# Priority for the copies of a four-chunk recurrence, and two pinned VectorE steps, in a hybrid decoder layer

## The chip, the cores and the metric

One core of one Trainium2 chip runs one layer of a decoder for a prompt of 256 tokens and 8 single-token samples together (264 columns). The metric is the device time of the kernel in microseconds (us). The engines of the core run side by side, each through its own queue in a fixed order: TensorE (PE in the profile), VectorE (DVE), ScalarE (ACT), GpSimd (POOL), and SyncE (SP), which here only issues transfers.

## What is computed

The layer is a half-step SwiGLU network, a mixing stage, and a second half-step network. The mixing stage has windowed attention for half of the width and an RWKV-7 recurrence for the other half. The change touches the recurrence alone:

```python
def step(S, inp):
    r_t, lw_t, k_t, v_t, kk_t, a_t = inp
    sa = jnp.einsum('bhij,bhj->bhi', S, -kk_t)
    S = (S * jnp.exp(lw_t)[:, :, None, :] + sa[..., None] * (kk_t * a_t)[:, :, None, :]
         + v_t[..., None] * k_t[:, :, None, :])
    return S, jnp.einsum('bhij,bhj->bhi', S, r_t)
```

16 heads of width 64 run through it. The rest of the layer is matrix products in float32 accuracy: `x + 0.5 * swiglu(norm(x))`, then `x + mixed @ w_out`, then the second network.

## The kernel before

Every weight product is made of *chunks* of 128 x 512 weights (`chunk` and `gemm`). SyncE loads a chunk into `raw` (6 buffers); ScalarE casts it to `hi`; VectorE subtracts it to get `lo` (4 buffers each; in a part of the mixing stage GpSimd makes every second `lo`). TensorE then makes 12 products of 128 x 264 per chunk into an accumulator `acc`, three for each of the chunk's four tiles: `hi` by the high part of the activations, `hi` by the low part, `lo` by the high part. So a `lo` that comes late stops TensorE, and because VectorE works in order, so does whatever stands ahead of that `lo` in VectorE's queue.

The recurrence is done in four chunks of 64 tokens, for two pairs of heads at a time: four *batches*, each a generator (`chain`). The generators advance by one `yield` with each weight chunk of the mixing stage (`tick`), so that their small instructions are traced between the chunks. For each batch:

1. Once `prep` has written the masked products `gm` to a DRAM scratch (`sa`), `chain` loads them back as `X` and `Xt` (`Y` in the code), waits 8 steps, and inverts 32 x 32 triangles on VectorE: for s = 1 to 30 a product `st` and an addition into `Xt`, each addition waiting for its product and each product for the addition before it. These 60 instructions are called the *inverse* below.
2. `Xt` goes to DRAM (`sb`) and comes back as `TT`; after 8 more steps two VectorE transpositions make `TN` from it.
3. TensorE multiplies with `TN`, ScalarE copies the result (`zs`), TensorE multiplies again, ScalarE copies into `TT`.
4. TensorE makes `pW` and `pU`. ScalarE copies `pW` to `W`; VectorE copies one half of `pU` to `uv`, ScalarE the other half. TensorE makes `pP`, `pG` from `W` and `pN`, `pY` from `uv`. ScalarE copies `pP` to `PT`; VectorE adds `pG` into `KR` (`kr`) and scales `pN` into `N`.
5. Three steps over the chunks, c = 1, 2, 3: TensorE multiplies the state `S` (at first a part of `N`) by `PT`; VectorE makes `Z`, then the next `S`.

The order in which instructions stand on each engine is not the traced one: a scheduler with its own timeline model orders them, by priority and by when it takes them to be ready. `tc.high_priority()` raises the instructions in its block; the loads, casts and `lo` of the weight chunks have it already. `tc.keep_in_program_order(i)` forbids that `i` stands ahead of the instruction that was traced before it on its engine. The inverse of one batch runs on VectorE at about the time at which the steps 3 to 5 of the batch before it run on the other engines.

Of the kernel before, what the change touches and what calls it, by code (L numbers as in the profile page):

```python
# [10 lines left out]
ALU = mybir.AluOpType  # L11
AX = mybir.AxisListType

P = 128
# [10 lines left out]
HALF = (slice(0, 64), slice(64, 128))  # L25
# [8 lines left out]
DWAIT = (8, 8, 8, 8)  # L34
# [13 lines left out]
def body(tc, I, O):  # L48
    nc = tc.nc
    V, A, G, TE, SP = nc.vector, nc.scalar, nc.gpsimd, nc.tensor, nc.sync  # L50
# [6 lines left out]
    def tt(e, out, a, b, op):  # L57
        return e.tensor_tensor(out=out, in0=a, in1=b, op=op)  # L58

    def stt(out, a, s, b, op0, op1):  # L60
        return V.scalar_tensor_tensor(out=out, in0=a, scalar=s, in1=b, op0=op0, op1=op1)  # L61
# [8 lines left out]
    def bc(ap, shape):  # L70
        return ap.broadcast_to(list(shape))

    def mm(out, lhsT, rhs, start=True, stop=True, **k):
        TE.matmul(out, lhsT, rhs, start=start, stop=stop, **k)  # L74
# [16 lines left out]
    def pause(n):  # L91
        for _ in range(n):
            yield

    with ExitStack() as ctx:
# [14 lines left out]
        def acc():  # L110
            return pp.tile([P, 512], F32, tag="acc", bufs=NACC, name=uid("acc"))

        def mp():
            return pp.tile([P, 512], F32, tag="m", bufs=NM, name=uid("m"))
# [243 lines left out]
        def mixing_body(mx, n2, n3, XD):  # L358
            def fix(shape, name):
                return mx.tile(list(shape), F32, name=name)  # L360

            def ring(shape, tag, bufs):
                return mx.tile(list(shape), F32, tag=tag, bufs=bufs, name=uid(tag))
# [9 lines left out]
            wc = fix((P, NPAIR, 4), "wc")  # L373
# [18 lines left out]
            def win(t):  # L392
                ps = acc()
                gemm(ps, I["win"][t], n2.xs, tick, share=t >= LKV + 4)
                if not have[0]:
                    n2.rstd(rs)
                    have[0] = True
                return ps
# [141 lines left out]
            def newbatch(i):  # L540
                bt = Batch()
                n = BATCH[i]
                bt.i, bt.n, bt.left, bt.p0 = i, n, n, sum(BATCH[:i])
                bt.KR, bt.bv = [None] * n, [None] * n
                bt.Gm = [[None, None] for _ in range(n)]
                bt.BT = [None] * n
                bt.UV = ring((P, 4, n, P), "uv", NUV)
                return bt

            def chain(bt):  # L550
                n = bt.n
# [7 lines left out]
                X = ring((ng * nr, 32, 32), "X", 1)  # L559
                Y = ring((ng * nr, nj, 32), "Xt", 1)  # L560
# [4 lines left out]
                TT = ring((P, n * 4, 64), "TT", NTT)  # L565
# [3 lines left out]
                for s in range(1, 31):  # L569
                    m, w = -(-s // ng), 31 - s  # L570
                    t = ring((ng * nr, m, w), "st", 2)
                    shp = (ng * nr, m, w)
                    tt(V, t, bc(X[:, s:s + 1, s + 1:], shp), bc(Y[:, :m, s:s + 1], shp), ALU.mult)
                    tt(V, Y[:, :m, s + 1:], Y[:, :m, s + 1:], t, ALU.add)
                    if s % NSTEP == 0:
                        yield
# [6 lines left out]
                for h in range(2):  # L583
                    for blk in range(2):
                        x = h * 64 + blk * 32
                        SP.dma_start(TT[x:x + 32, :, blk * 32:blk * 32 + 32],
                                     scr2[bt.i].rearrange("(h b m) (s t) -> h b s m t", h=2, b=2, s=32)[h, blk])
                yield from pause(DWAIT[bt.i])
                TN = ring((P, n * 4, 32), "TN", 1)
                for h in range(2):  # L590
                    V.transpose(TN[h * 64:h * 64 + 32], TT[h * 64:h * 64 + 32, :, 0:32])
                yield
                def sub(h, x):
                    return slice(h * 64 + x * 32, h * 64 + x * 32 + 32)
# [1 line left out]
                def quads(k):  # L596
                    return slice(k * 4, k * 4 + 4), slice(k * P, k * P + P)

                ps = mp()
# [7 lines left out]
                for k in range(n):  # L607
                    c, x = quads(k)
# [3 lines left out]
                ps = mp()  # L612
# [5 lines left out]
                for k in range(n):  # L618
                    c, x = quads(k)
# [4 lines left out]
                uv = bt.UV  # L624
                W, PT = ring((P, n, 3, 64), "W", 1), ring((P, n, 3, 64), "PT", 1)
                N = ring((P, n, 4, 64), "N", 1)
                pW, pU = mp(), mp()
# [6 lines left out]
                                    mm(ps[HALF[h ^ m], j * 64:j * 64 + 64], TT[HALF[h], j, :],  # L634
                                       bt.KR[k][HALF[h], a, c, :])
                pW, pU = (ps.rearrange("p (k c t) -> p k c t", k=n, c=4) for ps in (pW, pU))
                A.copy(W, pW[:, :, 1:4, :])
                V.tensor_copy(uv[HALF[0], :, :, HALF[0]].rearrange("p c k t -> p k c t"), pU[HALF[1]])
                A.copy(uv[HALF[1], :, :, HALF[1]].rearrange("p c k t -> p k c t"), pU[HALF[0]])
                yield  # L640
                pP, pG = mp(), mp()
                for k in range(n):
# [6 lines left out]
                            r = HALF[h]  # L649
                            mm(pG[r, x:x + 64], W[r, k, c - 1, :], bt.Gm[k][h][r, c, 64:128])  # L650
                pP, pG = (ps[:, :n * 192].rearrange("p (k c t) -> p k c t", k=n, c=3) for ps in (pP, pG))
                for h in range(2):
                    A.copy(PT[HALF[h]], pP[HALF[1 - h]])
                for k in range(n):
                    tt(V, bt.KR[k][:, 1, 1:4, :], pG[:, k], bt.KR[k][:, 1, 1:4, :], ALU.add)
                pN, pY = mp(), mp()
                for k in range(n):
                    for c in range(4):
# [4 lines left out]
                for k in range(n):  # L663
                    for c in range(4):
                        x = (k * 4 + c) * 64
                        for h in range(2):
                            r = HALF[h]
                            mm(pY[HALF[1 - h], x:x + 64], uv[:, c, k, r], bt.Gm[k][h][:, c, 64:128],
                               k + c == 0, c == 0, skip_group_check=True)
                tt(V, N, pN[:, :n * 256].rearrange("p (k c t) -> p k c t", k=n, c=4),  # L670
                   bc(wc[:, bt.p0:bt.p0 + n, :].unsqueeze(3), (P, n, 4, 64)), ALU.mult)
                yield
                S = N[:, :, 0, :]
                for c in range(1, 4):
                    ps = mp()
                    for k in range(n):
                        for h in range(2):
                            r = HALF[h]
                            mm(ps[r, k * 64:k * 64 + 64], PT[r, k, c - 1, :], S[r, k])
                        for h in range(2):  # L680
                            r = HALF[h]
                            x = (k * 4 + c) * 64
                            mm(pY[HALF[1 - h], x:x + 64], S[r, k], bt.KR[k][r, 1, c, :], False, True,
                               skip_group_check=True)
                    Z, Sn = ring((P, n, 64), "Z", 2), ring((P, n, 64), "S", 3)
                    for k in range(n):
                        stt(Z[:, k], S[:, k], wc[:, bt.p0 + k, c:c + 1], N[:, k, c, :], ALU.mult, ALU.add)
                    for k in range(n):
                        stt(Sn[:, k], ps[:, k * 64:k * 64 + 64], wc[:, bt.p0 + k, c:c + 1], Z[:, k], ALU.mult, ALU.add)
                    S = Sn  # L690
                    yield
                for k in range(n):
# [12 lines left out]
                for k in range(n):  # L705
                    p, o = bt.p0 + k, Ys[k]
# [169 lines left out]
            for kind, i in SEQ:  # L876
                if kind == "b":
                    bt = newbatch(i)
                    for k in range(BATCH[i]):
                        p = bt.p0 + k  # L880
                        x = [shifted(2 + 3 * p + j, tmp()) for j in range(3)]
                        spawn(prep(p, bt, k, *x))
                    bat.append(spawn(chain(bt)))
                    bts.append(bt)
                    if len(bat) == len(BATCH):
                        A.dma_start(O["sh"], shc)
                elif kind == "kv":
                    w, p = i // 2, i % 2
                    ps = win(LKV + i)
# [5 lines left out]
                else:  # L895
                    ps = win(LKV + 4 + i)
# [5 lines left out]
                    if i % 4 == 3:  # L902
                        p = i // 4
# [20 lines left out]
            for pi, ks in enumerate(PASS):  # L924
# [5 lines left out]
                for o in range(KD):  # L930
                    ps = acc()
# [160 lines left out]
```

## Time and profile before

| | us |
|---|---|
| three runs | 2001.56, 2002.91, 2004.8 |
| profiled execution, its own time | 2001.57 |
| its span, first to last instruction | 1999.8 |
| TensorE busy in the span | 1969.5 |
| VectorE busy | 1301.4 |
| ScalarE busy | 1065.4 |

The profiled execution is the fastest of the runs; what lies around its span is 1.8 us. The first network ends at about 769 us, and the mixing stage ends at about 1235 us. The views that follow are parts of the profile's page, the waits, sums over windows of time, and timelines of one engine. A timeline's row has the start in us, the duration in us, engine, line, operation, what is written and what is read, the shape, and how many equal instructions the row holds; in brackets stands the idle time of the engine before it and what ended that. TensorE's rows overlap, since its products are pipelined: how long a group holds the engine is read from its start to the next group's start. A program matmul of float32 operands shows as two rows' worth of instructions in the profile (x2), one of the `acc` products as one.

### The profile page before, as it was taken

Reading aid. Unit: us, or ns where it says so; the run is one execution under the profiler, and the core shown is the slowest. Engines: PE = TensorE matmul, PEld = TensorE weight load, DVE = VectorE, ACT = ScalarE, POOL = GpSimd, SP = SyncE. Lnnn points to the kernel's source line nnn. Section 1 sums busy time; section 2 is a strip of 40 time slices with the busy share of each in tenths; the row PEclk is TensorE's granted clock in tenths of the full one; section 3 lists DMA queues with packets and bytes.
Section 4 is the critical chain, followed back from the end, with each engine's and each line's share of the span. In section 5 each row is a group of like instructions: output and inputs, shape, how many; then the busy total and the mean of one; then the engine's idle time right before and its main releaser. Section 6 shows DMA issues by size and latency. Waiting matters only on the chain.

```text
span 1999.8 us, 45897 instructions
## 1 busy us (share of the span) xinstructions
PE 1969.5 (98%) x17212; PEld 1933.6 (97%) x17212; DVE 1301.4 (65%) x2546; ACT 1065.4 (53%) x2137; POOL 343.1 (17%) x437
## 2 busy tenths in 40 slices
PE   9999999999999999998998999999999999999998
PEld 9999999999999999997987899999999999999997
DVE  5865555655556577687867676765666666666665
ACT  5644444444444456775666765654444444444445
POOL 0401001010010121121124553120101001010012
PEclk9999999999999999999999999999999999999999
DMA  7666666655556667554555546565666666666654
GB/s 230 178 190 194 185 192 191 184 184 176 187 178 184 181 196 222 160 148 121 155 144 148 162 144 196 174 181 178 187 190 192 181 190 194 184 192 183 195 179 146
DMA packets 229232, 358.77 MB, mean 179 GB/s; under 512 B 42616, under 2 KB 84240, under 8 KB 229008
## 3 DMA queue, kind: packets, MB, share of 16 engines
q1 hardware_dynamic: 223120, 349.72, 57.9%
q10 hardware_dynamic: 5888, 6.11, 1.0%
q8 instruction: 135, 2.21, 0.4%
q14 instruction: 89, 0.73, 0.1%
HBM read 347.59 MB, written 10.22 MB: 179 GB/s over the span
## 4 chain that ended last, share of the span: by engine, by line
PE 91%; DVE 4%; DMA 2%; ACT 1%; issue 1%; SPq 1%; POOL 0%; ACTq 0%; DVEq 0%; POOLq 0%
PE acc L74 84%; PE m L74 6%; DVE lo L58 1%; DMA raw<-in_gu 1%; DVE st L58 1%; DVE Xt L58 1%; DMA raw<-in_win 0%; ACT t L68 0%; ACT hi L127 0%; DMA sb<-Xt 0%; DMA TT<-sb 0%; DVE y L58 0%; SPq L562 0%; DMA Xt<-sa 0%; SPq L563 0%
## 5 line engine op out<-in xcount | busy, mean ns | idle before, releaser
L127 ACT CAST hi<-raw 128x512 fp32r<-128x512 f32 (+2 forms) x1304 | 778.5, 601 | 818.0 <-PE acc L74 725.1
L58 DVE TENSOR_TENSOR lo<-raw,hi 128x512 fp32r<-128x512 f32 (+1 forms) x1248 | 854.4, 688 | 535.8 <-ACT hi L127 512.0
L74 PE MATMUL acc<-s,hi 128*128 128x264 f32 x5940 | 1111.7, 286 | 1.1 <-ACT hi L127 1.1
L74 PEld LDWEIGHTS acc<-s,hi 128*128 128x128 f32 x5940 | 923.3, 188 | 8.4 <-ACT hi L127 1.8
L74 PE MATMUL acc<-s,lo 128*128 128x264 f32 x2970 | 848.2, 286 | 4.9 <-DVE lo L58 4.6
L74 PEld LDWEIGHTS acc<-s,lo 128*128 128x128 f32 x2970 | 558.4, 188 | 9.5 <-DVE lo L58 6.4
L74 PE MATMUL acc<-t,hi 128*128 128x264 f32 x2752 | 502.8, 284 | 0.0
L74 PEld LDWEIGHTS acc<-t,hi 128*128 128x128 f32 x2752 | 425.9, 188 | 0.0
L74 PE MATMUL acc<-t,lo 128*128 128x264 f32 x1376 | 388.5, 284 | 0.0
L58 POOL TENSOR_TENSOR t<-t,t 128x264 f32<-128x264 f32 (+1 forms) x148 | 150.8, 1019 | 1148.6 <-ACT hi L127 789.9
L74 PEld LDWEIGHTS acc<-t,lo 128*128 128x128 f32 x1376 | 258.1, 188 | 0.1
L74 PE MATMUL acc<-y,hi 128*128 128x264 f32 x648 | 123.9, 284 | 0.0
L74 PEld LDWEIGHTS acc<-y,hi 128*128 128x128 f32 x648 | 101.2, 188 | 0.2
L74 PE MATMUL acc<-y,lo 128*128 128x264 f32 x324 | 91.3, 282 | 0.0
L58 DVE TENSOR_TENSOR t<-acc,t 128x264 f32<-128x264 f32 x156 | 67.4, 432 | 35.9 <-PE acc L74 35.7
L58 POOL TENSOR_TENSOR lo<-raw,hi 128x512 fp32r<-128x512 f32 x56 | 75.4, 1347 | 63.3 <-ACT hi L127 36.9
L58 POOL TENSOR_TENSOR o<-o,o 128x264 f32<-128x264 f32 x43 | 36.5, 848 | 187.4 <-ACT o L68 181.7
L74 PE MATMUL acc<-o,hi 128*128 128x264 f32 x324 | 62.4, 282 | 0.0
L74 PEld LDWEIGHTS acc<-y,lo 128*128 128x128 f32 x324 | 60.9, 188 | 0.0
L61 DVE SCALAR_TENSOR_TENSOR s<-acc,s 128x264 f32<-128x264 f32 x96 | 40.6, 428 | 15.9 <-PE acc L74 15.5
L74 PEld LDWEIGHTS acc<-o,hi 128*128 128x128 f32 x324 | 50.0, 188 | 0.0
L74 PE MATMUL m<-s,hi 128*128 128x264 f32 x260 | 48.1, 285 | 0.0
(252 smaller groups left out, 1336.9 us busy)
## 6 DMA issues: line engine op xcount, KB each, us to landing
raw<-in_gu SPq DMA_DIRECT2D x688, 256.0 KB, 3.4
raw<-in_dn SPq DMA_DIRECT2D x224, 256.0 KB, 2.9
raw<-in_win SPq DMA_DIRECT2D x152, 256.0 KB, 3.5
raw<-in_dn SPq DMA_DIRECT2D x160, 192.0 KB, 2.7
raw<-in_wout SPq DMA_DIRECT2D x48, 256.0 KB, 3.3
raw<-in_wout SPq DMA_DIRECT2D x32, 128.0 KB, 3.1
s<-xsp SPq DMA_DIRECT2D x16, 132.0 KB, 3.9
ld<-in_sT SPq DMA_DIRECT2D x16, 128.0 KB, 3.6
```

The lines of the kernel that those rows point to most:

```text
L58: return e.tensor_tensor(out=out, in0=a, in1=b, op=op)
L61: return V.scalar_tensor_tensor(out=out, in0=a, scalar=s, in1=b, op0=op0, op1=op1)
L74: TE.matmul(out, lhsT, rhs, start=start, stop=stop, **k)
L127: A.copy(hi[:, :w], raw[:, :w])
```

## The change

The diff does these things, all in `chain`:

- The first product of each inverse (s = 1) and the two transpositions to `TN` are kept in program order on VectorE, and the transpositions are traced two steps earlier than before (a pause of 6 instead of 8).
- Both halves of `pU` are copied by ScalarE; VectorE's copy of the first half is gone.
- `W` and the two copies to `uv`, the two copies to `PT`, the additions into `kr`, the scaling to `N`, and the two instructions that make each `S` have high priority. (`Z` has not.)

```diff
--- before.py
+++ after.py
@@ -570,7 +570,9 @@
                     m, w = -(-s // ng), 31 - s
                     t = ring((ng * nr, m, w), "st", 2)
                     shp = (ng * nr, m, w)
-                    tt(V, t, bc(X[:, s:s + 1, s + 1:], shp), bc(Y[:, :m, s:s + 1], shp), ALU.mult)
+                    first = tt(V, t, bc(X[:, s:s + 1, s + 1:], shp), bc(Y[:, :m, s:s + 1], shp), ALU.mult)
+                    if s == 1:
+                        tc.keep_in_program_order(first)
                     tt(V, Y[:, :m, s + 1:], Y[:, :m, s + 1:], t, ALU.add)
                     if s % NSTEP == 0:
                         yield
@@ -585,10 +587,10 @@
                         x = h * 64 + blk * 32
                         SP.dma_start(TT[x:x + 32, :, blk * 32:blk * 32 + 32],
                                      scr2[bt.i].rearrange("(h b m) (s t) -> h b s m t", h=2, b=2, s=32)[h, blk])
-                yield from pause(DWAIT[bt.i])
+                yield from pause(DWAIT[bt.i] - 2)
                 TN = ring((P, n * 4, 32), "TN", 1)
                 for h in range(2):
-                    V.transpose(TN[h * 64:h * 64 + 32], TT[h * 64:h * 64 + 32, :, 0:32])
+                    tc.keep_in_program_order(V.transpose(TN[h * 64:h * 64 + 32], TT[h * 64:h * 64 + 32, :, 0:32]))
                 yield
                 def sub(h, x):
                     return slice(h * 64 + x * 32, h * 64 + x * 32 + 32)
@@ -634,9 +636,10 @@
                                     mm(ps[HALF[h ^ m], j * 64:j * 64 + 64], TT[HALF[h], j, :],
                                        bt.KR[k][HALF[h], a, c, :])
                 pW, pU = (ps.rearrange("p (k c t) -> p k c t", k=n, c=4) for ps in (pW, pU))
-                A.copy(W, pW[:, :, 1:4, :])
-                V.tensor_copy(uv[HALF[0], :, :, HALF[0]].rearrange("p c k t -> p k c t"), pU[HALF[1]])
-                A.copy(uv[HALF[1], :, :, HALF[1]].rearrange("p c k t -> p k c t"), pU[HALF[0]])
+                with tc.high_priority():
+                    A.copy(W, pW[:, :, 1:4, :])
+                    for h in range(2):
+                        A.copy(uv[HALF[h], :, :, HALF[h]].rearrange("p c k t -> p k c t"), pU[HALF[1 - h]])
                 yield
                 pP, pG = mp(), mp()
                 for k in range(n):
@@ -649,10 +652,11 @@
                             r = HALF[h]
                             mm(pG[r, x:x + 64], W[r, k, c - 1, :], bt.Gm[k][h][r, c, 64:128])
                 pP, pG = (ps[:, :n * 192].rearrange("p (k c t) -> p k c t", k=n, c=3) for ps in (pP, pG))
-                for h in range(2):
-                    A.copy(PT[HALF[h]], pP[HALF[1 - h]])
-                for k in range(n):
-                    tt(V, bt.KR[k][:, 1, 1:4, :], pG[:, k], bt.KR[k][:, 1, 1:4, :], ALU.add)
+                with tc.high_priority():
+                    for h in range(2):
+                        A.copy(PT[HALF[h]], pP[HALF[1 - h]])
+                    for k in range(n):
+                        tt(V, bt.KR[k][:, 1, 1:4, :], pG[:, k], bt.KR[k][:, 1, 1:4, :], ALU.add)
                 pN, pY = mp(), mp()
                 for k in range(n):
                     for c in range(4):
@@ -667,8 +671,9 @@
                             r = HALF[h]
                             mm(pY[HALF[1 - h], x:x + 64], uv[:, c, k, r], bt.Gm[k][h][:, c, 64:128],
                                k + c == 0, c == 0, skip_group_check=True)
-                tt(V, N, pN[:, :n * 256].rearrange("p (k c t) -> p k c t", k=n, c=4),
-                   bc(wc[:, bt.p0:bt.p0 + n, :].unsqueeze(3), (P, n, 4, 64)), ALU.mult)
+                with tc.high_priority():
+                    tt(V, N, pN[:, :n * 256].rearrange("p (k c t) -> p k c t", k=n, c=4),
+                       bc(wc[:, bt.p0:bt.p0 + n, :].unsqueeze(3), (P, n, 4, 64)), ALU.mult)
                 yield
                 S = N[:, :, 0, :]
                 for c in range(1, 4):
@@ -685,8 +690,10 @@
                     Z, Sn = ring((P, n, 64), "Z", 2), ring((P, n, 64), "S", 3)
                     for k in range(n):
                         stt(Z[:, k], S[:, k], wc[:, bt.p0 + k, c:c + 1], N[:, k, c, :], ALU.mult, ALU.add)
-                    for k in range(n):
-                        stt(Sn[:, k], ps[:, k * 64:k * 64 + 64], wc[:, bt.p0 + k, c:c + 1], Z[:, k], ALU.mult, ALU.add)
+                    with tc.high_priority():
+                        for k in range(n):
+                            stt(Sn[:, k], ps[:, k * 64:k * 64 + 64], wc[:, bt.p0 + k, c:c + 1], Z[:, k],
+                                ALU.mult, ALU.add)
                     S = Sn
                     yield
                 for k in range(n):
```

The computation is the same. What moves, engine by engine, is the scheduler's answer. Three places, all as they stand in each engine's queue; numbers behind names tell buffers apart and differ between the two programs.

TensorE in the second batch, between `pY` (`m` from `gm` and `uv`) and the first product that reads `N`. Before, from the first `acc` product behind `pY`:

```order
L74 MATMUL acc_14439<-s_10421,hi_14560 128x264
L74 MATMUL acc_14439<-s_10420,lo_14561 128x264
L74 MATMUL acc_14439<-s_10463,hi_14560 128x264
L74 MATMUL acc_14439<-s_10464,hi_14560 128x264
L74 MATMUL acc_14439<-s_10463,lo_14561 128x264
L74 MATMUL acc_14439<-s_10506,hi_14560 128x264
L74 MATMUL acc_14439<-s_10507,hi_14560 128x264
L74 MATMUL acc_14439<-s_10506,lo_14561 128x264
L74 MATMUL acc_14439<-s_10549,hi_14560 128x264
L74 MATMUL acc_14439<-s_10550,hi_14560 128x264
L74 MATMUL acc_14439<-s_10549,lo_14561 128x264
L74 MATMUL m_14259<-N_14076,PT_14075 64x64 x2
```

With the change, from the last product of `pY`:

```order
L74 MATMUL m_14113<-gm_12503,uv_11362 64x64
L74 MATMUL acc_14270<-s_10120,hi_14327 128x264
L74 MATMUL acc_14270<-s_10119,lo_14328 128x264
L74 MATMUL m_14175<-N_14010,PT_14009 64x64 x2
L74 MATMUL m_14113<-kr_11881,N_14010 64x64 x2
```

Between `pY` and the first product with `N` stood eleven `acc` products; now two stand there.

VectorE in the second batch, the stretch that ends with `N`; the `st` and `Xt` rows belong to the inverse of the third batch. Before:

```order
L58 TENSOR_TENSOR lo_14686<-raw_14684,hi_14685 128x512
L58 TENSOR_TENSOR st_14517<-X_13672,Xt_13673 128x60
L58 TENSOR_TENSOR Xt_13673<-Xt_13673,st_14517 128x6x10
L58 TENSOR_TENSOR st_14520<-X_13672,Xt_13673 128x54
L58 TENSOR_TENSOR kr_11881<-m_14164,kr_11881 128x192
L58 TENSOR_TENSOR kr_12312<-m_14164,kr_12312 128x192
L58 TENSOR_TENSOR Xt_13673<-Xt_13673,st_14520 128x6x9
L58 TENSOR_TENSOR st_14553<-X_13672,Xt_13673 128x48
L58 TENSOR_TENSOR Xt_13673<-Xt_13673,st_14553 128x6x8
L58 TENSOR_TENSOR N_14076<-m_14193,wc 128x512
```

With the change:

```order
L58 TENSOR_TENSOR st_14525<-X_13672,Xt_13673 128x60
L58 TENSOR_TENSOR kr_11881<-m_14083,kr_11881 128x192
L58 TENSOR_TENSOR kr_12312<-m_14083,kr_12312 128x192
L58 TENSOR_TENSOR Xt_13673<-Xt_13673,st_14525 128x6x10
L58 TENSOR_TENSOR st_14528<-X_13672,Xt_13673 128x54
L58 TENSOR_TENSOR Xt_13673<-Xt_13673,st_14528 128x6x9
L58 TENSOR_TENSOR st_14553<-X_13672,Xt_13673 128x48
L58 TENSOR_TENSOR Xt_13673<-Xt_13673,st_14553 128x6x8
L58 TENSOR_TENSOR st_14556<-X_13672,Xt_13673 128x42
L58 TENSOR_TENSOR Xt_13673<-Xt_13673,st_14556 128x6x7
L58 TENSOR_TENSOR N_14010<-m_14112,wc 128x512
```

`N` still stands behind the inverse's rows, now behind one more pair of them (those of width 42). Over a longer stretch, from the first `t` that reads the product `m` of 128 x 280 columns (made just ahead of `pW`) to `N`, there were four `lo` and are now one.

ScalarE in the first batch, from the activation or copies ahead of `W`. Before:

```order
L127 CAST hi_13301<-raw_13300 128x512
L68 ACTIVATE t_12855<-pj_10571,vec 128x256
L637 COPY W_12986<-m_12989 128x384
L516 COPY kr_12737<-m_13028 64x2x64 x4
L523 COPY BT_13040<-m_13035 128x4x64
L525 COPY BT_13040<-m_13035 64x4x64
L639 COPY uv_10754<-m_12990 64x2x4x64
L525 COPY BT_13040<-m_13035 64x4x64
```

With the change:

```order
L623 COPY TT_11738<-m_12839 32x4x32 x4
L489 COPY XD<-m_12869 128x2x4
L491 COPY XD<-m_12870 64x2x4 x2
L640 COPY W_12920<-m_12923 128x384
L642 COPY uv_10754<-m_12924 64x2x4x64 x2
L657 COPY PT_12921<-m_12994 64x384 x2
```

`W`, both copies to `uv` and both copies to `PT` now follow each other; before, nine copies of the next pair's preparation (`kr`, `BT`) stood among them.

## The prediction

> **What bounds the kernel now.** I read the page's first table and its chain of waits, then sums over windows, then TensorE's timeline for the rows that waited, then VectorE's around them.
>
> ```profile
> span 1999.8 us, 45897 instructions
> PE 1969.5 (98%) x17212; PEld 1933.6 (97%) x17212; DVE 1301.4 (65%) x2546; ACT 1065.4 (53%) x2137; POOL 343.1 (17%) x437
> PE 91%; DVE 4%; DMA 2%; ACT 1%; issue 1%; SPq 1%; POOL 0%; ACTq 0%; DVEq 0%; POOLq 0%
> 68.50 700.18 PE acc L74 x5760
> ```
>
> TensorE is busy for 98% of the span, and the chain of waits is 91% TensorE. Its last row here, 5760 products in one run of 700.18 us without another engine in it, gives the price of an `acc` product: 0.1216 us, so a chunk of 12 takes 1.46 us. Only TensorE's pauses can be won or lost. The mixing stage in windows (length, busy time of PE, PEld, DVE, ACT, POOL, then PE's granted clock, DMA share, GB/s):
>
> ```profile
> 840.00:900.00 60.00, 59.24 (x555) 56.57 (x554) 46.33 (x134) 46.33 (x113) 13.23 (x31) 1.00 0.56 153
> 900.00:935.00 35.00, 28.78 (x438) 25.66 (x438) 28.95 (x102) 16.63 (x45) 6.37 (x16) 0.90 0.43 116
> 935.00:990.00 55.00, 52.71 (x555) 49.15 (x554) 42.22 (x98) 37.69 (x95) 10.99 (x25) 1.00 0.54 152
> 990.00:1010.00 20.00, 19.21 (x322) 17.63 (x324) 17.50 (x68) 12.30 (x30) 1.17 (x7) 1.00 0.49 140
> 1010.00:1050.00 40.00, 37.81 (x435) 34.52 (x436) 25.37 (x53) 24.60 (x63) 12.53 (x18) 1.00 0.54 144
> 1050.00:1065.00 15.00, 10.33 (x182) 9.60 (x180) 14.05 (x62) 8.12 (x22) 5.89 (x6) 1.00 0.56 178
> 1065.00:1180.00 115.00, 113.86 (x1160) 97.97 (x1159) 81.25 (x250) 77.19 (x222) 58.36 (x65) 1.00 0.48 143
> 924.30:931.10 6.80, 5.48 (x102) 5.25 (x103) 6.26 (x26) 3.10 (x8) 0.10 (x1) 0.50 0.16 39
> ```
>
> TensorE's idle time is length less busy: 0.76, 6.22, 2.29, 0.79, 2.19, 4.67 and 1.14 us, together 18.1. Inside the second window stands a stretch at half clock: its 5.48 busy us would be 2.74 at full clock, so it cost 2.7. All that the change can win is thus 20.8 us, about 1%. The rows that waited:
>
> ```profile
> 902.75 0.39 PE L74 MATMUL acc<-s,lo 128*128 128x264 f32 x1 [1.19 <-DVE lo L58]
> 907.52 0.39 PE L74 MATMUL acc<-s,lo 128*128 128x264 f32 x1 [1.81 <-DVE lo L58]
> 922.12 0.45 PE L74 MATMUL m<-uv,gm 64*64 64x64 f32 x8 [1.13 <-ACT W L637]
> 925.62 0.59 PE L74 MATMUL m<-gm,W 64*64 64x64 f32 x6 [1.97 <-ACT uv L639]
> 1002.85 0.27 PE L74 MATMUL m<-N,PT 64*64 64x64 f32 x2 [0.79 <-DVE st L58]
> 1054.69 0.27 PE L74 MATMUL m<-BT,W 64*64 64x64 f32 x2 [2.12 <-ACT W L637]
> ```
>
> The first two come from `lo` behind a transposition or a first product that waits for a transfer; the others are the recurrence's own waits, which the change aims at: `W`, `uv`, `N`.
>
> **The change part by part.** *Copies on ScalarE.* In the first batch `W` stood behind an activation that waited for VectorE, and the second `uv` copy behind `kr` and `BT` copies and behind VectorE's own `uv` copy. The new order puts `W`, both `uv` and both `PT` in one row on ScalarE. That removes 1.13 + 1.97 in batch 0 and the half clock behind it, 2.7: 5.8. The copy that leaves VectorE (0.61 us, from 996.24 to 996.85 in a fence below) returns on ScalarE, which is busy for 16.63 of that window's 35 us. I cost it at nothing, because TensorE's next real wait is for `N` and the copy ends well before; if that cover were gone, it would cost its 0.6 us in each of four batches, 2.4. Queued behind it on ScalarE are the casts to `hi`; they lose nothing while TensorE itself stands still.
>
> *N, where the change does not do what it says.* Its priority brings `N` past three `lo`, but not past the next batch's inverse: 19 pairs of `st` and `Xt` still stand between `t` and `N` on VectorE, about as many as before. The new order also moves TensorE's side. Both sides, in batch 1, from the product of 280 columns just ahead of `pW`:
>
> ```profile
> 985.36 0.64 PE L74 MATMUL m<-t,C 128*128 128x280 f32 x2
> 985.92 0.64 PE L74 MATMUL m<-XD,ld 64*64 64x2 f32 x32
> 986.50 0.45 PE L74 MATMUL m<-TN,gm 32*32 32x32 f32 x32
> 986.88 1.49 PE L74 MATMUL m<-kr,bk 64*128 64x128 f32 x16
> 988.29 0.40 PE L74 MATMUL acc<-s,hi 128*128 128x264 f32 x1
> 992.49 1.15 PE L74 MATMUL m<-kr,TT 64*64 64x64 f32 x56
> 993.57 0.44 PE L513 MATMUL m<-C,kr 128*128 128x128 f32 x2
> 997.22 0.56 PE L74 MATMUL m<-BT,W 64*64 64x64 f32 x12
> 998.44 1.15 PE L74 MATMUL m<-uv,BT 128*64 128x64 f32 x32
> 999.42 1.10 PE L74 MATMUL m<-gm,uv 128*64 128x64 f32 x32
> 1000.46 0.39 PE L74 MATMUL acc<-s,hi 128*128 128x264 f32 x1
> ```
>
> TensorE's own steps that remain between that product and the first with `N`, from start to next start: 0.56 + 0.58 + 1.41 + 1.08 + 1.22 + 0.98 + 1.04 = 6.87 us. Among them stood 53 `acc` products before, 6.44 us; now there are 9, 1.09 us (12 in batch 0, 1.46). So TensorE comes to `N` after 7.96 us (8.33 in batch 0), where the same two sums were 13.3 before, with further steps between them that now come earlier. VectorE's side:
>
> ```profile
> 987.95 0.42 DVE L58 TENSOR_TENSOR t<-m,t 128x264 f32<-128x264 f32 x1
> 996.24 0.69 DVE L638 COPY uv<-m 64x512 f32<-64x512 f32 x1
> 996.85 0.21 DVE L58 TENSOR_TENSOR Xt<-Xt,st 128x60 f32<-128x60 f32 x1
> 997.24 0.68 DVE L58 TENSOR_TENSOR lo<-raw,hi 128x512 fp32r<-128x512 f32 x1
> 997.85 0.22 DVE L58 TENSOR_TENSOR Xt<-Xt,st 128x70 f32<-128x70 f32 x1
> 998.11 0.23 DVE L58 TENSOR_TENSOR st<-X,Xt 128x65 f32<-128x65 f32 x1
> 1002.02 0.68 DVE L58 TENSOR_TENSOR N<-m,wc 128x512 f32<-128x512 f32 x1
> ```
>
> From `t` to the end of `N` (1002.70) it took 14.75 us for 51 rows. The new order has 48: three `lo` fewer (0.61 each, 997.24 to 997.85), no `uv` copy (0.61), and one `s` against one `t` of the same size. 14.75 - 1.83 - 0.61 = 12.3 us, most of it the inverse. `t` cannot start before the product of 280 columns ends, 0.56 us in; so `N` is there 12.9 us after that product's start at the earliest, and TensorE, with 0.15 us for the hand-over (1002.70 to 1002.85), idles 13.0 - 8.0 = 5.0 us. Before, VectorE came to `t` 2.0 us after the product's end, which gives 7.0; later still, 9. I take 6.5, less the 0.79 that stood there: +5.7. While TensorE waits, everything behind it waits too: the `acc` products, and with them the buffers of `raw`, `hi` and `lo`, so nothing else is done in that time. Behind the first products with `N` only seven `acc` products (0.85 us) and four short groups stand ahead of the first that reads `S`, where VectorE needs this long to make `S`:
>
> ```profile
> 1004.84 0.47 DVE L61 SCALAR_TENSOR_TENSOR S<-m,wc,Z 128x64 f32<-128x64 f32 x2
> ```
>
> From the end of `N` at 1002.70 to the end of `S` at 1005.31 are 2.6 us, with rows of the inverse between, as there are now. That leaves a wait of 0 to 2, taken as +1. In batch 0 TensorE comes after 8.33 us; on VectorE no `lo` is left (0.6 less), but 22 pairs stand there instead of 19, and a pair costs 0.26 to 0.52 us (0.26 is 997.85 to 998.11 for one of its two instructions, and short work fits between them): 12.6 to 13.4. The idle is then 5.0 to 7.8; taken as 6.3, less the 5.8 removed: +0.5.
>
> *The pinned steps.* The third inverse's first product waits for its load:
>
> ```profile
> 976.54 0.19 DVE L58 TENSOR_TENSOR st<-X,Xt 128x30 f32<-128x30 f32 x1 [2.75 <-DMA Xt<-sa]
> 980.25 0.39 PE L74 MATMUL acc<-s,lo 128*128 128x264 f32 x1 [0.85 <-DVE lo L58]
> ```
>
> It now stands two `lo` earlier, and nothing in the order brings the load forward. Two chunks are 2.9 us of TensorE; the two `lo` behind the wait are 1.2 us of VectorE that is no longer spent ahead of it, so the wait grows by 1.7 and 1.8 us more reach TensorE (0 if `Xt` lands sooner, 2.9 at most). The transposition of batch 1 goes the other way, two `lo` later, with its transfer behind two more weight loads on SyncE: of the 1.19 + 1.81 us between none and all returns. Together with the 2.29 and 2.19 us of `lo` waits in the windows 935 to 990 and 1010 to 1050, whose places shift, I take -1 (from -4 to +3). The 0.76 us of the first window goes: -0.7.
>
> *Batch 2.* Its inverse is further done when its chain runs, and `W` no longer stands behind softmax. Of 4.67 us idle I give it 1 (from -3 to +1, as `N` still stands behind an inverse). Batch 3 has none behind it: 0.
>
> *Clock.* Two long idles where before one stretch lost 2.7. The 1050 to 1065 window idled 4.67 us and kept a clock of 1.00, so no idle time is certain to bring half clock: 0 to 5.4, taken as +1.5.
>
> Sum: +0.5 (batch 0) + 8.5 (batch 1: 5.7 + 1 + 1.8) - 1 (pinned, others) - 0.7 - 1 (batch 2) + 1.5 = +7.8. The profiled execution's own time is 2001.57, 1.3 below the median of 2002.91; with that, 2001.6 + 7.8 + 1.3 = 2010.7, said as **2010**.
>
> **Rivals.** *The waits vanish as meant.* If VectorE reaches `N` within 8 us of the product of 280 columns, because the inverse runs further ahead than the order shows, 1.13 + 1.97 + 0.79 + 4.67 + 2.7 = 11.3 go: 1992. For it speaks that VectorE does three `lo` fewer; against it the 22 pairs that still stand ahead of `N`, each waiting for nothing but the one before it. It decides from an idle time under 1 us before `N` in batch 1.
>
> *The waits only move.* Batch 0 gains 3, batch 2 gains 3, the clock stays open, and batch 1's idle is at its low end, 5.0 - 0.8 + 1 = 5.2, with the pinned load hidden; with -0.7 and -1 that is -2.5 or, with the clock's 1.5, -1: 2000.4 to 2001.9, about 2001.5. The spare time of VectorE in 935 to 990 (42.22 of 55 us busy) speaks for it.
>
> *The gate closes.* Each long idle brings a stretch like 924.30 to 931.10, 2.7 us: 5.4 for the 1.5 in the sum, 2014.6. For it: that stretch came when the longest idle was 1.97 us, and 5 to 7 are expected. Against it: 1050 to 1065. [...]
>
> **How the numbers follow.** Forecast 0.50, the gate 0.15, waits only move 0.18, waits vanish 0.17. The forecast's own range is 2004 to 2016: batch 1 between 6 and 11, the rest as bounded. Over all, 2000 to 2018: it leaves out the last case and some 0.03 above. A measurement of this kernel tells a change from none at about 0.2%, 4 us, so no change is 1999 to 2007. Slower: nearly all of the first two and a little of the third, 0.66; the same: most of the third, a little of the first, 0.16; faster: 0.18.
>
> **What would show it.** In the profile after: an idle of 5 us or more on TensorE before the product of `N` and `PT` in batches 0 and 1, ended by VectorE; `W` and `uv` no longer among the long waits; the `lo` wait at the third inverse's first product above 2 us. Wrong, if VectorE comes to `t` with the inverse nearly done, or if the `lo` that left this stretch are what TensorE misses later.

## The result, and the profile after

| | before | with the change |
|---|---|---|
| median of 7 runs, us | 2002.91 (2000.76 to 2004.8) | 2009.9 (2007.8 to 2011.35) |
| ratio | 1 | 1.0033, 95% interval [1.0022, 1.0045] |
| span of the profiled execution, us | 1999.8 | 2008.3 |
| TensorE busy, us | 1969.5 | 1969.2 |

The change makes the kernel slower by about 7 us. TensorE does the same work and shows the same busy time, so by the profile's sums the 8.5 us between the spans are TensorE standing still. The page of the changed kernel, its first lines and the shares of its chain of waits:

```profile
span 2008.3 us, 45907 instructions
PE 1969.2 (98%) x17212; PEld 1934.5 (96%) x17212; DVE 1306.8 (65%) x2542; ACT 1074.0 (53%) x2145; POOL 340.3 (17%) x437
PE 93%; DVE 3%; DMA 2%; SPq 1%; ACT 1%; issue 1%; POOL 0%; DVEq 0%; ACTq 0%
```

The same seven windows of the mixing stage as in the prediction (length, busy time of PE, PEld, DVE, ACT, POOL, PE's granted clock, DMA share, GB/s):

```profile
840.00:900.00 60.00, 60.00 (x566) 57.61 (x564) 48.82 (x137) 47.05 (x113) 13.71 (x34) 1.00 0.57 161
900.00:935.00 35.00, 27.21 (x448) 23.98 (x449) 27.95 (x103) 15.88 (x46) 4.17 (x13) 0.90 0.34 89
935.00:990.00 55.00, 50.12 (x602) 46.62 (x602) 40.40 (x95) 39.47 (x97) 12.38 (x27) 1.00 0.54 154
990.00:1010.00 20.00, 13.65 (x188) 12.22 (x189) 14.45 (x59) 8.20 (x21) 0.32 (x3) 0.83 0.28 65
1010.00:1050.00 40.00, 39.91 (x401) 37.23 (x400) 26.80 (x43) 26.14 (x64) 10.20 (x17) 1.00 0.56 163
1050.00:1065.00 15.00, 10.01 (x214) 9.13 (x212) 11.84 (x42) 7.17 (x14) 4.98 (x7) 0.97 0.52 154
1065.00:1180.00 115.00, 111.73 (x1140) 96.81 (x1141) 84.10 (x272) 83.11 (x233) 55.42 (x65) 0.97 0.49 144
```

Length less busy gives 0, 7.79, 4.88, 6.35, 0.09, 4.99 and 3.27 us of idle time, 27.4 together, where there were 18.1: 9.3 more, which covers the 8.5. The window 990 to 1010, the second batch's chain, went from 0.79 to 6.35. TensorE's rows that waited longest:

```profile
908.18 0.73 PE L74 MATMUL m<-t,C 128*128 128x280 f32 x2 [1.90 <-POOL t L58]
917.21 1.97 PE L74 MATMUL m<-gm,uv 128*64 128x64 f32 x32 [3.01 <-DVE gm L58]
923.96 0.30 PE L74 MATMUL m<-N,PT 64*64 64x64 f32 x2 [2.80 <-DVE Xt L58]
979.67 0.39 PE L74 MATMUL acc<-s,lo 128*128 128x264 f32 x1 [2.17 <-DVE lo L58]
986.59 1.51 PE L74 MATMUL m<-kr,bk 64*128 64x128 f32 x16 [1.91 <-ACT XD L489]
999.02 0.37 PE L74 MATMUL m<-N,PT 64*64 64x64 f32 x2 [5.92 <-DVE st L58]
1065.48 1.62 PE L74 MATMUL m<-s,o 64*128 64x256 f32 x6 [5.47 <-DVE Xt L58]
```

`W` and `uv` are no longer waited for; `N` is, and it is named by VectorE's instruction just ahead of it, a `st` or `Xt` of the inverse. VectorE in the second batch, the first and the last row of the stretch:

```profile
985.83 0.42 DVE L58 TENSOR_TENSOR t<-m,t 128x264 f32<-128x264 f32 x1
998.07 0.20 DVE L58 TENSOR_TENSOR Xt<-Xt,st 128x42 f32<-128x42 f32 x1
998.19 0.68 DVE L58 TENSOR_TENSOR N<-m,wc 128x512 f32<-128x512 f32 x1
```

From `t` to the end of `N` at 998.79 (the next row's start) are 13.0 us, forecast 12.3. On TensorE the product of 280 columns starts at 982.39 and the work ahead of `N` ends at 993.10. That is 10.7 us, 2.3 of it waits (1.91 and 0.42), so 8.4 of work, forecast 7.96. TensorE reached `N` early and VectorE late, as forecast. *Why* it came to stand so is another matter.

### The profile page after: what moved, and what is told of

The parts are those of the page before. It is cut to its first block, busy times and chain, and to the rows that moved or that the text cites. A ratio compares the mean times of both kernels' runs of the same rounds, so it can differ in the third digit from the quotient of the medians.

```text
span 2008.3 us, 45907 instructions
## 1 busy us (share of the span) xinstructions
PE 1969.2 (98%) x17212; PEld 1934.5 (96%) x17212; DVE 1306.8 (65%) x2542; ACT 1074.0 (53%) x2145; POOL 340.3 (17%) x437
## 4 chain that ended last, share of the span: by engine, by line
PE 93%; DVE 3%; DMA 2%; SPq 1%; ACT 1%; issue 1%; POOL 0%; DVEq 0%; ACTq 0%
PE acc L74 86%; PE m L74 7%; DVE Xt L58 1%; DVE st L58 1%; DVE lo L58 0%; DMA raw<-in_gu 0%; DMA Xt<-sa 0%; DMA X<-sa 0%; DMA xg<-in_xT 0%; SPq L563 0%; PE m L520 0%; DVE t L61 0%; SPq L126 0%; DVE y L58 0%; ACT hi L127 0%
## 5 line engine op out<-in xcount | busy, mean ns | idle before, releaser
L61 DVE SCALAR_TENSOR_TENSOR s<-acc,s 128x264 f32<-128x264 f32 x96 | 40.6, 428 | 15.9 <-PE acc L74 15.5
```

## The experiments

Two facts come from the order of instructions alone. The kernel before with high priority for `kr`, `N` and `S` has the same order on all five engines as without it, buffer numbers aside. The kernel with every priority of the change has the same order as with its `uv` copies alone, and the whole change without any of its priorities has the order of the whole change. So the priorities do nothing here: they are no cause. That leaves three parts: both `uv` copies on ScalarE, the two pins, and the second pause, 6 instead of 8.

**Pause 8, no pins** (what stays: `uv` on ScalarE and the priorities).

```diff
-                    if s == 1:
-                        tc.keep_in_program_order(first)
-                yield from pause(DWAIT[bt.i] - 2)
+                yield from pause(DWAIT[bt.i])
-                    tc.keep_in_program_order(V.transpose(...))
+                    V.transpose(...)
```

> The changed kernel with the second pause back at 8 and both pins gone; what stays of the change is both uv copies on ScalarE and every priority. The prediction's theory (the priority of N and of the copies takes the acc products away from in front of N): N is still waited for by 5 us or more in batches 0 and 1, time 2007 to 2011. Rival (the shorter pause, not the priority, moved TensorE's order): 27 acc products stand between the products with TT and N as before, the N waits stay below 3 us, time 1998 to 2005.

Measured: 2005.55 us, ratio 1.0007 [0.9999, 1.0016]. The loss is gone, so the forecast's theory fails here; the rival's time and its 3 us for `N` are both missed by a little. Any gain of the copies is gone too. TensorE still waits 1.13 us for `W`, and for `N` 1.39 and 3.41 us in the first and third batch: what the copies gave in one place was waited for in the next.

**The pause of 6 alone**, on the kernel before.

```diff
-                yield from pause(DWAIT[bt.i])
+                yield from pause(DWAIT[bt.i] - 2)
```

> The kernel before with one edit: the second pause is 6 instead of 8; no priority, no pin, uv as before. The prediction's theory: nothing of the loss without the priorities, time 2000 to 2005. Rival (the pause alone): the idle before N in batch 1 is 4 us or more, VectorE runs 20 pairs of the inverse ahead of N, time 2007 to 2013.

Measured: 2031.18 us, ratio 1.0128 [1.0115, 1.0141]. One line that traces the transposition two steps earlier costs 26 us, more than either theory gave it. Its waits on TensorE (what was waited for, us in total, times, longest):

```profile
PE m L74 <- DVE Xt L58: 9.7, 2, 5.3
PE acc L74 <- DVE lo L58: 4.4, 5, 1.4
PE m L74 <- DVE S L61: 4.2, 3, 2.0
PE m L74 <- ACT zs L610: 4.0, 1, 4.0
PE m L74 <- DVE mxv L777: 3.4, 1, 3.4
```

The first row is `N` behind the inverse in two batches. In this kernel's order VectorE has up to 20 products of the inverse behind the last `lo` ahead of `N`, where the kernel before has at most 4. Standing still is only about half of the loss: between 840 and 1180 TensorE idles 34.7 us, before 18.1, and it runs at half clock for 47.8 us in eight stretches, before 6.8 in one. Its busy time grew from 1969.5 to 1983.3 us.

**The whole change with the pause at 8.**

```diff
-                yield from pause(DWAIT[bt.i] - 2)
+                yield from pause(DWAIT[bt.i])
```

> The whole change, pins and priorities included, with the second pause at 8. If the pins cost time by themselves (VectorE held at a transfer with lo behind it), 2006 to 2010 with lo waits above 2 us at the inverses' first products. If the pause alone is the cause, 1997 to 2005.

Measured: 1999.0 us, ratio 0.9972 [0.9961, 0.9982]. The change without its shorter pause is a gain of 5.6 us. Pins and all, the pause of 6 is worth 1.0033 against 0.9972, some 12 us.

**The whole change, with each product of the inverse in program order.** The pause is 6, and TensorE's order ahead of `N` is that of the change.

```diff
-                    if s == 1:
-                        tc.keep_in_program_order(first)
+                    tc.keep_in_program_order(first)
```

> The whole change, pause of 6 included, with each product of the inverse kept in program order on VectorE (the change keeps the first only), so that 1 to 4 pairs stand ahead of N instead of 10 to 22. TensorE's side is as in the change: 9 to 12 acc products. If the inverse ahead of N is what TensorE waits for: the 5.9 us idle in batch 1 falls below 2, the gate stays open there, time 1996 to 2004. If N is late for another reason (its own steps on TensorE and ScalarE): the idle stays above 4, time 2007 or more.

Measured: 1996.94 us, ratio 0.9967 [0.9954, 0.998]. VectorE and TensorE in the second batch:

```profile
982.24 0.42 DVE L58 TENSOR_TENSOR t<-m,t 128x264 f32<-128x264 f32 x1
986.13 1.29 DVE L58 TENSOR_TENSOR gm<-m,C 128x512 f32<-128x512 f32 x2 [1.93 <-PE m L74]
988.45 0.62 DVE L58 TENSOR_TENSOR kr<-m,kr 128x192 f32<-128x192 f32 x2 [1.03 <-PE m L74]
989.49 0.69 DVE L58 TENSOR_TENSOR N<-m,wc 128x512 f32<-128x512 f32 x1 [0.41 <-PE m L74]
```

```profile
980.02 1.30 PE L74 MATMUL m<-t,C 128*128 128x280 f32 x2
990.74 0.27 PE L74 MATMUL m<-N,PT 64*64 64x64 f32 x2
```

`t` to the end of `N` takes 7.9 us instead of 13.0, VectorE now waits for TensorE, and the product with `N` has no idle time ahead of it. The same 9 `acc` products stand on TensorE as in the change, so taking the inverse out of the way ends the wait. Against the expectation the clock did fall here: TensorE ran at half clock from 980.0 to 986.8 (6.8 us, granted clock 0.50), behind waits for `TN` and `zs` (1.03 and 1.97 us). The product of 280 columns took 1.30 us in it, and 0.64 at a granted clock of 1.00 in the kernel before; taken as half of the 6.8, the fall lengthens TensorE's way to `N` by about 3.4 us, an estimate. But VectorE waits 1.93 + 1.03 + 0.41 us for TensorE in the same stretch, so at full clock it would hardly have had to wait for VectorE either. So the wait for `N` is the inverse ahead of it; this is shown.

**The two pins alone**, at both pauses, with `uv` and priorities as before.

```diff
+                    if s == 1:
+                        tc.keep_in_program_order(first)
-                    V.transpose(...)
+                    tc.keep_in_program_order(V.transpose(...))
```

> The kernel before with the two pins and nothing else: pause 8, no priority, uv copied as before. If the gain of the change with pause 8 (0.9972) comes from the pins, 1997 to 2001. If it needs both uv copies on ScalarE, 2002 to 2007.

> The kernel before with the two pins and the pause of 6: the change without its uv copies and its priorities. If priorities and uv copies are worth nothing measurable here, within 3 us of the change, 2008 to 2014. If they help or hurt, outside of that.

Measured: pause 8, 1999.21 us, 0.9973 [0.9963, 0.9983]; pause 6, 2008.25 us, 1.0020 [1.0011, 1.0030]. Beside the kernels with `uv` on ScalarE and the priorities (0.9972 and 1.0033) the copies bring nothing at pause 8, and at pause 6 the difference is about 1 part in 1000 against them, with intervals that overlap. The pins bring 0.3% at pause 8 and take the pause of 6 from 1.0128 to 1.0020; which of the two does that at pause 6 was not tried.

**Each pin alone**, pause 8.

```diff
+                    if s == 1:
+                        tc.keep_in_program_order(first)
```

> The kernel before with the pin on the first product of each inverse alone, pause 8. Both pins together gave 0.9973. If this pin is the one that gains (VectorE no longer stands at the load of X and Xt ahead of lo): 1997 to 2001. If it is the transposition's: 2002 to 2007, and the lo waits of 1.19 and 1.81 us ahead of the second batch stay.

```diff
-                    V.transpose(...)
+                    tc.keep_in_program_order(V.transpose(...))
```

> The kernel before with the pin on the two transpositions alone, pause 8. If this pin is the one that gains, 1997 to 2001 and the lo waits of 1.19 and 1.81 us are gone; if not, 2002 to 2007. If each pin carries a part, both single kernels lie between, 2000 to 2003.

Measured: the first product's pin 1998.77 us, 0.9975 [0.9966, 0.9984]; the transposition's 2001.7 us, 0.9992 [0.9983, 1.0001]. All of the gain that can be told from noise is the first product's. In the kernel before, VectorE stood 2.69 us at the second inverse's first product, with `lo` behind it:

```profile
906.33 0.19 DVE L58 TENSOR_TENSOR st<-X,Xt 128x30 f32<-128x30 f32 x1 [2.69 <-DMA raw<-in_win]
```

With the pin alone, at the same place:

```profile
904.04 0.19 DVE L58 TENSOR_TENSOR st<-X,Xt 128x30 f32<-128x30 f32 x1 [0.85 <-DMA Xt<-sa]
```

The wait is 1.8 us shorter, and TensorE's 1.81 us for `lo` at 907.52 has gone; of the pair 1.19 and 1.81 a single 1.25 is left. This place is a part of the gain only: TensorE's idle time between 840 and 1180 fell from 18.1 to 11.6 us, and the rest of it was not taken apart.

**The inverse in order, with other pauses.** Pause 8, with and without the transposition's pin, then 7 and 9; each is the whole change with every product of the inverse in order. The kernel without the transposition's pin also leaves out the priorities of `kr`, `N` and `S`.

```diff
-                yield from pause(DWAIT[bt.i] - 2)
+                yield from pause(DWAIT[bt.i] + 1)
```

> The whole change with the pause back at 8 and each product of the inverse kept in program order. If the pairs ahead of N and the short cover on TensorE are two separate costs, both gone here: 1988 to 1995, no wait for N above 1 us in any batch. If one already removes what the other would: 1995 to 2000.

> As the kernel with the inverse in order and the pause of 8, but the transposition to TN not pinned. If the pin on the transposition is what saves the lo waits ahead of the second batch (1.19 and 1.81 us before), 2 to 5 us more than with it. If the first product's place alone does it, within 1.5 us.

> The whole change with each product of the inverse in order and the second pause at 7. Between the kernels with 6 (0.9967) and 8 (0.9957): with the inverse out of the way the pause should matter by 3 us at most, 1993 to 1999. If the pause costs by itself, 6 and 7 lie above 8 and 9 by 2 us or more.

> The same with the pause at 9. If a later chain is still better, 1990 to 1994, below the kernel with 8. If 8 is the best place, 1995 to 2000, with the chain of the last batch ending nearer to the end of the mixing stage.

| pause | us | ratio |
|---|---|---|
| 6 | 1996.94 | 0.9967 [0.9954, 0.998] |
| 7 | 1997.54 | 0.997 [0.996, 0.9981] |
| 8 | 1995.22 | 0.9957 [0.9945, 0.997] |
| 8, transposition not pinned | 1995.23 | 0.9961 [0.9949, 0.9974] |
| 9 | 1987.61 | 0.9921 [0.9907, 0.9934] |

The two rows with 8 have the same order on all five engines, so they are one program measured twice. With the inverse in order, 6 to 8 lie together within their intervals, 9 below them: the 12 us between the pauses of 6 and 8 shrink to less than 2, so the shorter pause costs through the inverse that it leaves ahead of `N`. The two costs are not separate. At 8 there is no long wait for `N` in the first three batches, but TensorE waits for `W` instead (1.07 and 2.46 us). The kernel with 9 is the best of all, 16 us below the kernel before and below what was expected of it; a pause of 9 without the inverse in order was not tried. Its two longest kinds of wait:

```profile
PE acc L74 <- DVE lo L58: 2.6, 4, 1.0
PE m L74 <- DVE N L58: 1.6, 2, 1.2
```

No single wait of its mixing stage is longer than 1.2 us. Why 9 gains so much over 8 (7.6 us) is open: TensorE's idle time over 0.4 us between 840 and 1260 falls only from 9.6 to 8.1 us, while its busy time in the span falls from 1971.5 to 1965.2 us.

## Why the prediction was right, and where not

The time was forecast at 2010 (the sum gave 2010.7) and is 2009.9, and the mechanism that was forecast is there: `N` behind the inverse, with too little left on TensorE to cover it. But several terms were off and cancelled, and one cause was named wrongly. From the first window to the last:

| term | forecast, us | in the profile after |
|---|---|---|
| first window's `lo` wait | -0.7 | 0.76 to 0 |
| batch 0, idle ahead of `N` | 6.3 | 2.80, and 3.01 at `pY`, ended by `gm` on VectorE |
| batch 1, idle ahead of `N` | 6.5 | 5.92, and 0.42 at `pY` |
| batch 1, wait for `S` | 1 | none |
| batch 1, `lo` behind the third inverse's first product | 0.85 + 1.8 | 0.67 + 2.17 |
| pinned steps and other `lo` waits | -1 | 1.19 + 1.81 gone; 1010 to 1050 from 2.19 to 0.09 |
| waits for GpSimd's `t` and for `XD` | none | 1.90 and 1.91 |
| batch 2 | 4.67 - 1 | 5.47 in one wait |
| half clock | +1.5 | three more stretches, see below |

*Right:* the two-sided reckoning of `N`, TensorE at 8 us and VectorE at 13. It rests on counts of the new order times durations of the old trace, and the parts held within 0.7 us. The wait itself, 5.92 for 6.5, is the rest of two further shifts that work against each other: VectorE came to `t` 3.4 us after the product's start (2.6 in the kernel before), and TensorE lost 2.3 us on its way to waits that no term had. In batch 0 the forecast's own sign, 5 us or more before the product of `N`, is not there: 2.80 stand there, 3.01 earlier.

*Luck, the total.* In idle time the forecast's terms add up to +9.0 us (3.2 for batch 0, 5.7, 1, 1.8, -1, -0.7, -1), and the windows show +9.3. But the two waits of 1.90 and 1.91 are in no term, and 5.1 us went where 1 was forecast. The clock was to give back 1.2 (2.7 saved, 1.5 spent); half clock grew instead from 6.8 to 20.5 us. That the time came within 1 us is partly luck.

*Wrong, the cause.* The step "N, where the change does not do what it says" took it that `N`'s priority brought it past three `lo` and that the change's order as a whole moved TensorE's side. The priorities move nothing. The pause of 6 moves both sides: it alone gives 1.0128, and the whole change without it 0.9972. The diff had four parts, and the forecast asked only for their joint order; the order of each part alone, at hand before any run, would have shown it.

*Wrong, what the pins do.* "The pinned steps" charged the first pin with +1.8 us and took -1 for the rest. The `lo` waits at the third inverse did grow as forecast (2.84 against 2.65), but not by the pin. The kernel with the pause of 6 and no pin stands there too, with `lo` waits of 1.39 and 1.14 us on TensorE behind it:

```profile
983.84 0.19 DVE L58 TENSOR_TENSOR st<-X,Xt 128x30 f32<-128x30 f32 x1 [5.33 <-DMA Xt<-sa]
```

The kernel before stood 2.75 us at this product. With the first product's pin alone, at pause 8, VectorE stands 1.37 us and TensorE waits for no `lo` there; the whole change at pause 8 has one such wait, of 1.19 us. So most of the growth came with the pause. A forbidden early place is here first of all a wait saved where the load is late: the first product's pin gains 0.25% at pause 8, and at pause 6 the two save some 22 us of a loss that the forecast did not know of.

*Misread, the other `lo` waits.* The same step calls the 2.29 and 2.19 us of 935 to 990 and 1010 to 1050 waits for `lo`. Of the first 0.85 is, and of the second nothing: 1.68 of it is a wait for an activation, in the profile before:

```profile
1022.89 0.71 PE L74 MATMUL m<-sgl,ld 128*128 128x264 f32 x2 [1.68 <-ACT t L68]
```

*Mis-sized, batch 2.* "I give it 1": it idled 5.47 instead of 4.67. VectorE's row that ends just ahead, at 1065.25, is the addition into `kr`, which reads `pG`, behind the inverse of the last batch; that the waiting product needed the buffer of `pG` is read from the place, not tried.

*Half clock.* The change has these stretches, where the kernel before had one:

```profile
917.20:920.90 3.70, 3.69 (x41) 3.57 (x41) 3.32 (x15) 0.00 (x0) 0.00 (x0) 0.54 0.11 18
924.10:927.50 3.40, 3.40 (x34) 2.83 (x33) 3.09 (x16) 2.15 (x7) 0.32 (x3) 0.50 0.00 0
995.60:1002.60 7.00, 3.58 (x34) 3.05 (x35) 6.23 (x31) 2.14 (x7) 0.32 (x3) 0.51 0.26 90
1064.00:1070.70 6.70, 5.22 (x34) 4.52 (x35) 6.43 (x35) 0.88 (x4) 0.39 (x2) 0.50 0.50 138
```

15.9 us of TensorE's busy time fell into them, before 5.48. Half of the difference is 5.2, about what the rival "the gate closes" gave (5.4), and the clock did fall, to 0.50, in or just behind each of the four longest idles (5.92, 5.47, 3.01 and 2.80 us). Yet the busy time of the whole span did not grow, and the 9.3 us of idle time already cover the 8.5. TensorE's small groups stand in another arrangement in the two programs, and pipelined rows overlap (a product of 280 columns shows 0.64 us where the next row starts 0.56 later), so about 5 us of busy time must have gone elsewhere; where is left open.

*The rivals.* "The waits vanish" needed VectorE at `N` within 8 us of the product of 280 columns. The kernel with the inverse in order comes nearest: `N` starts 9.5 us after that product's start, most of them at half clock, and the time is 1997, not 1992. It has the pins too, so it is no test of that rival's price. "The waits only move" is what `uv` on ScalarE does by itself: 1.0007.

## What to carry to other kernels

Where a scheduler sets the order, take the change apart and look at the order of each part before reasoning on the sum: here the priorities moved nothing, and the pause, one line among many, cost the most. A value that the bottleneck waits for is as late as the independent work that a scheduler has put ahead of it on an in-order engine; keeping that filler in program order took the change from 1.0033 to 0.9967, where the priority on the value did nothing. (At pause 8 the same edit takes it from 0.9972 to 0.9957, with intervals that overlap.) And a first step that waits for a load is better held back to its place in the program, since everything behind it on its engine waits with it (in the kernel before 2.69 us on VectorE, with 1.81 us on TensorE for the `lo` behind it): here that gave 0.25%.

## What the runs showed of the hardware

In the kernel before, TensorE's granted clock fell to 0.50 behind idle times that were short and in pieces: the 3.4 us ahead of the half-clock stretch were busy for 1.63. At 1050.60 TensorE was busy for 1.98 of 3.40, and the clock stayed:

```profile
920.90:924.30 3.40, 1.63 (x24) 1.16 (x23) 3.13 (x14) 2.67 (x8) 1.52 (x4) 1.00 0.25 75
1050.60:1054.00 3.40, 1.98 (x17) 1.76 (x15) 3.16 (x18) 3.40 (x14) 1.61 (x2) 1.00 0.83 272
```

In the changed kernel the clock fell at 917.2, 924.1, 995.8 and 1064.0. Its stretches at half clock in the mixing stage hold 3.41, 3.41, 6.83 and 6.83 us, summed from the granted clock over windows of 0.5 us; the one of the kernel before holds 6.83. How much idle time brings half clock is not settled: 1.98 us of work in 3.40 kept the clock above, and in the kernel with the inverse in order and a pause of 9 it fell behind 2.52 of 3.41:

```profile
1020.25:1023.66 3.41, 2.52 (x45) 2.21 (x44) 3.38 (x11) 1.11 (x4) 0.77 (x1) 1.00 0.54 164
1023.66:1027.07 3.41, 3.41 (x22) 3.19 (x20) 3.34 (x15) 0.77 (x3) 0.73 (x2) 0.50 0.78 195
```

What brings half clock was not tried by itself.
